# A first adaLN half in two quarters: the start of a decoder trunk layer on one Trainium2 core

## The chip, the core and the metric

The kernel runs on one core of a Trainium2 chip. A core has five engines with a queue of instructions each: TensorE (PE in the profile, its weight loads PEld), VectorE (DVE), ScalarE (ACT), GpSimd (POOL) and SyncE (SP, which here only issues DMAs). Each works through its own queue in order and waits on semaphores for the others. The metric is the device time of one execution in microseconds, the median of several runs.

## The reference

One layer of a decoder trunk, for a prompt of 512 tokens and 8 samples of one token that share the weights, all in f32:

```
sh1, sc1, g1, sh2, sc2, g2 = split(silu(c) @ ada_w + ada_b, 6)     # adaLN: 1024 -> 6 x 1024, 9 condition rows
h = rms_norm(x, norm1_g) * (1 + sc1) + sh1
xr, gr, q, k, v, fl, ga, gb = split(h @ w_in)
ya = (RG-LRU(conv(xr)) * gelu(gr)) @ w_proj_a
yb = attention_with_forget_gates(q, k, v, fl) @ w_proj_b           # samples: over a paged cache
x = x + g1 * ((sigmoid(ga) * ya + sigmoid(gb) * yb) @ w_o)
x = x + g2 * SwiGLU(rms_norm(x, norm2_g) * (1 + sc2) + sh2)
y = rms_norm(x, normf_g)
```

What matters here is the beginning: nothing of `h @ w_in` can start before the columns of sh1 and sc1 that belong to the first rows of h are known.

## The kernel before

Activations lie transposed: a tile holds 128 of the 1024 features on the partitions and all 520 tokens along the free axis, so x, xn and h are eight tiles each (f = 0 to 7). A product is made in two halves of 260 tokens (j = 0, 1). To reach f32 accuracy with the faster fp32r matmul, weights and activations are split into a high part (a cast on ACT: whi, hh) and a rest (a subtraction on DVE: wlo, hl), and three matmuls are summed for each k step: whi x hh, wlo x hh, whi x hl. A k step is one of the eight feature tiles.

The engines' queues are filled by a list scheduler that takes the program's instructions in the order of the code and moves them by its own estimate of when each is ready; `issue_after` and the tile pools' buffers set further bounds. The queues that come out are fixed; on the chip each engine works through its own in order.

The start of the kernel, in the order of the code:

1. x is loaded by SP (eight DMAs), ACT squares it, DVE adds the squares, PE sums them over the partitions (ss), ACT and DVE make 1/rms from it (r1).
2. `first_mod(0, ...)`: the first half of sh1 and sc1 (feature tiles 0 to 3 of both). For each of the eight k steps kq, SP loads 512 KB of ada_w (araw, a tile of the pool `pgp` with 7 buffers), and PE does four matmuls of 32 stationary columns (silc, the silu of the conditions) with 256 moving columns. The four write to four groups of 32 partitions of one bank, with `tile_position=(0, 32 * g)`. They are plain f32, and in the profile each shows as two instructions. From the third step on, `keep_busy` puts one full matmul with no use (idle) behind each step.
3. DVE makes xn = x * r1, eight tiles.
4. `q_weights`: SP loads a piece of q's weights (wraw), ACT and DVE split it. A piece is four k steps of two of q's output tiles.
5. `first_mod_end(0, ...)`: ACT copies the sums (adas), PE transposes them (adaft), with three idle matmuls behind it, and DVE adds the bias (mod) and makes the amplitude (n1amp).
6. `first_h(f)` for f = 0 to 3: ACT makes hh, POOL the eight sample columns, DVE the exact value (hr) and the rest hl.
7. q's first six output tiles over k steps 0 to 3, in two groups of three (`g3`), six banks each. In the first group the second adaLN half (`first_mod(1, ...)`) is put in two steps at a time behind each k step. Behind the first k step of the second group stands `first_mod_end(1, ...)` and `first_h` for f = 4 to 7.
8. Three more pieces of q's weights, then k steps 4 to 7 of the six tiles (L542 `q` in the profile, against `qp` for the steps before), and the rest of the kernel, the first parts of which load pages of the cache for the samples.

The hh and hl of tiles 4 to 7 and the last pieces of q's weights go through the same queues of ACT and DVE. The split weights (whi, wlo) have three buffers each, the pieces as loaded (wraw) two.

Of the kernel before, what the change touches and what calls it, by code (L numbers as in the profile page):

```python
# [8 lines left out]
F32 = mybir.dt.float32  # L9
# [3 lines left out]
ALU = mybir.AluOpType  # L13
# [11 lines left out]
KT = 8  # L25
# [10 lines left out]
P_N1, P_N2, P_NF, P_CW, P_CB, P_BR, P_BI, P_LAM = 0, 1, 2, 3, 7, 8, 9, 10  # L36
P_AB, P_SC, P_H0, P_C = 11, 17, 41, 49
# [28 lines left out]
def kernel(ctx, tc, xT, par, gates, b_f, cst, cse, own, cache_k, cache_v, cache_lf, pt,  # L66
# [3 lines left out]
    pe, act, dve, pool, sp = nc.tensor, nc.scalar, nc.vector, nc.gpsimd, nc.sync  # L70
# [9 lines left out]
    def slot(name, cols=NT, dt=F32, parts=128):  # L80
        return heap.tile([parts, cols], dt, name=name, tag="slot")

    def bank(name, parts=128, cols=512):
        return psp.tile([parts, cols], F32, name=name, tag="bank")
# [19 lines left out]
    ident = cs[:, C_ID:C_ID + 128]  # L104
# [371 lines left out]
    def first_mod(fh, acc, kqs):  # L476
        for kq in kqs:
            raw = pgp.tile([128, 2, 512], F32, name="araw", tag="pg")
            sp.dma_start(raw, ada_w[kq * 128:kq * 128 + 128, :2048].rearrange("p (v c) -> p v c", v=2)
                         [:, :, 512 * fh:512 * fh + 512])  # L480
            for g in range(4):
                m = pe.matmul(acc[32 * g:32 * g + 32, :256], lhsT=silc[:, kq],
                              rhs=raw[:, g // 2, 256 * (g % 2):256 * (g % 2) + 256],
                              start=kq == 0, stop=kq == KT - 1, tile_position=(0, 32 * g))
            if fh == 0:
                keep_busy(m, 1 if kq > 1 else 0)

    def keep_busy(m, n):
        for _ in range(n):
            with tc.issue_after(m.ins):  # L490
                m = pe.matmul(idle[:, :HALF], lhsT=ones, rhs=x[0][:, :HALF], start=True, stop=True)
# [53 lines left out]
    def wraw():  # L545
        return wp.tile([128, KT, 256], F32, name="wraw", tag="wraw", bufs=2)
# [3 lines left out]
    for f in range(KT):  # L550
# [6 lines left out]
        if f % 4 == 3:  # L557
            for j, (t0, t1) in enumerate(HALVES):
                pe.matmul(ssq[j][:, :HALF], lhsT=ones, rhs=sq[:, t0:t1], start=f == 3, stop=f == KT - 1)
    acc = [bank(f"adaf{fh}") for fh in range(2)]  # L560
    first_mod(0, acc[0], range(KT))
    r1 = slot("r1")
    for j, (t0, t1) in enumerate(HALVES):
        act.activation(r1[:, t0:t1], ssq[j][:, :HALF], AF.Sqrt, bias=eps, scale=1.0 / D)
        dve.reciprocal(r1[:, t0:t1], r1[:, t0:t1])
    for f in range(KT):
        t = slot("xn")
        dve.tensor_tensor(t, x[f], r1, ALU.mult)
        xn.append(t)
    raw = wraw()  # L570
    q_weights(0, raw, 0, 0)
    first_mod_end(0, acc[0])
    for f in range(4):
        first_h(f)
    q_weights(0, raw, 4, 2)
    raw = wraw()
    q_weights(0, raw, 0, 4)
    for g3 in (0, 3):
        banks = [bank(f"qp{i}_{j}") for i in range(g3, g3 + 3) for j in range(2)]
        for k in range(4):  # L580
            for n in range(6):
                q_matmuls(0, g3 + n // 2, n % 2, k, banks[n])
                if g3 == 0 and n == 5:
                    first_mod(1, acc[1], (2 * k, 2 * k + 1))
            if g3 and k == 0:
                first_mod_end(1, acc[1])
                for f in range(4, KT):
                    first_h(f)
        for n in range(6):
            t0, t1 = HALVES[n % 2]  # L590
            act.copy(qpart[g3 + n // 2][:, t0:t1], banks[n][:, :HALF])
        if g3 == 0:
            flr = slot("flr", KT * H).rearrange("p (k c) -> p k c", k=KT)
            sp.dma_start(flr, w_in[:, COL_FL:COL_FL + H].rearrange("(k p) c -> p k c", p=128))
# [1199 lines left out]
```

## Time and profile before

| | us |
|---|---|
| median of 3 runs | 1015.64 (1015.08 to 1018.36) |
| the profiled execution, its own time | 1018.03 |
| its span in the profile | 1016.4 |
| PE busy | 994.3 (98%) |
| DVE busy | 797.3 (78%) |
| ACT busy | 547.5 (54%) |
| POOL busy | 327.6 (32%) |
| first q matmul starts | 26.08 |
| first matmul of q's k steps 4 to 7 starts | 50.45 |

A row of the timeline gives start, duration, engine, line, operation, output<-inputs, shapes and a count of merged instructions; in brackets stands how long the engine had been idle and what released it. PE's ends are modelled, and its instructions overlap, so a distance between starts says more than a duration.

### The profile page before, as it was taken

The page shows a single profiled execution, that of the slowest core. Times are in us where ns is not written, and L with a number is a line of the kernel's source. Part 1 is how long each engine was busy: PE and PEld are TensorE (multiplying, and loading weights), DVE is VectorE, ACT ScalarE, POOL GpSimd, SP SyncE. Part 2 cuts the span into 40 slices and gives each one's busy share as a digit, 9 for nine tenths or more (in the row PEclk, how much of TensorE's full clock was granted, in tenths as well). Part 3 has the DMA queues.
Part 4 walks back from the last instruction along what each step waited for, and adds up shares of the span by engine and source line. Part 5 has one row for each costly group of instructions (what it writes and reads, how often), then busy time and mean ns, then how long its engine had stood idle before and what let it go on. Part 6 is the DMA issues. An engine that isn't in the chain of part 4 may idle for free.

```text
span 1016.4 us, 21281 instructions
## 1 busy us (share of the span) xinstructions
PE 994.3 (98%) x8012; PEld 921.1 (91%) x8012; DVE 797.3 (78%) x1423; ACT 547.5 (54%) x1128; POOL 327.6 (32%) x415
## 2 busy tenths in 40 slices
PE   5999999999999999999999999999999999999996
PEld 2799999999998988888888888999999999999996
DVE  5559999998999888886655544869988888888764
ACT  4534576848761576777783233554444444445553
POOL 0346111121143245653400001583442442425112
PEclk9999999999999999999999999999999999999998
DMA  9798857788879998995867995324234243233122
GB/s 325 250 324 279 242 189 202 243 261 278 281 250 345 331 312 286 321 294 190 251 216 269 319 340 186 84 74 115 81 108 125 63 125 98 70 104 105 63 64 85
DMA packets 164378, 206.97 MB, mean 204 GB/s; under 512 B 9827, under 2 KB 125043, under 8 KB 164211
## 3 DMA queue, kind: packets, MB, share of 16 engines
q1 hardware_dynamic: 147634, 152.78, 48.1%
q0 software_dynamic: 12960, 46.41, 13.8%
q10 hardware_dynamic: 3680, 6.42, 1.7%
q8 instruction: 63, 1.03, 0.4%
q14 instruction: 41, 0.33, 0.1%
HBM read 192.49 MB, written 13.09 MB: 202 GB/s over the span
## 4 chain that ended last, share of the span: by engine, by line
PE 93%; DMA 2%; DVE 2%; ACT 1%; issue 0%; SPq 0%; POOL 0%; DVEq 0%; POOLq 0%; ACTq 0%
PE fo L307 12%; PE k L307 5%; PE wo L307 5%; PE gb L307 5%; PE gr L307 5%; PE v L307 5%; PE ga L307 5%; PE xr L307 5%; PE pb L307 4%; PE pv L839 3%; PE pa L307 3%; PE po L1302 2%; PE qp L542 2%; PE q L542 2%; PE ada L374 2%; PE ptt L1268 2%
## 5 line engine op out<-in xcount | busy, mean ns | idle before, releaser
L246 ACT CAST whi<-wraw 128x1024 fp32r<-128x1024 f32 (+1 forms) x79 | 82.0, 1039 | 113.6 <-PE pb L307 34.3
L248 DVE TENSOR_TENSOR wlo<-wraw,whi 128x1024 fp32r<-128x1024 f32 (+1 forms) x79 | 99.1, 1256 | 19.0 <-ACT whi L246 16.6
L307 PE MATMUL fo<-ach,wb 128*128 128x260 f32 x512 | 93.4, 283 | 0.0
L270 ACT CAST wb<-ws 128x512 fp32r<-128x512 f32 x72 | 44.7, 621 | 86.0 <-PE fo L307 58.9
L700 POOL DMA_DIRECT2D pg<-in_cache_k_dram x74 | 39.6, 536 | 143.1 <-DVE S L751 62.6
L271 DVE TENSOR_TENSOR wb<-wraw,wb 128x512 fp32r<-128x512 f32 x86 | 76.4, 889 | 4.7 <-ACT wb L270 3.9
L307 PEld LDWEIGHTS fo<-ach,wb 128*128 128x128 f32 x512 | 78.9, 188 | 0.0
L271 DVE TENSOR_TENSOR wb<-ws,wb 128x512 fp32r<-128x512 f32 x72 | 68.7, 954 | 12.6 <-ACT wb L270 11.0
L261 POOL TENSOR_TENSOR ws<-wraw 128x512 f32<-128x512 f32 x18 | 24.4, 1353 | 153.2 <-DMA wraw<-in_w_fi_dram 104.1
L307 PE MATMUL fo<-acl,wb 128*128 128x260 f32 x256 | 72.2, 282 | 0.0
L270 ACT CAST wb<-wraw 128x512 fp32r<-128x512 f32 x86 | 53.5, 622 | 31.4 <-ACT cp L1683 6.2
L750 DVE TENSOR_TENSOR pg<-pg,qb 128x1024 f32<-128x1024 f32 x48 | 57.9, 1221 | 2.5 <-DMA pg<-in_cache_k_dram 2.5
L751 DVE TENSOR_REDUCE S<-pg 128x16 f32<-128x1024 f32 x48 | 57.4, 1209 | 0.2
L1259 POOL TENSOR_SCALAR p<-p,mu 128x128 f32<-128x128 f32 (+3 forms) x28 | 38.4, 1381 | 53.0 <-DVE mu L1255 47.1
L307 PEld LDWEIGHTS fo<-acl,wb 128*128 128x128 f32 x256 | 48.2, 188 | 0.0
L1253 ACT ACTIVATE p<-p,mu 128x128 f32<-128x128 f32 (+3 forms) x64 | 35.4, 554 | 18.2 <-DVE mu L1252 18.0
L307 PE MATMUL v<-hh,whi 128*128 128x260 f32 x128 | 38.2, 298 | 0.8 <-ACT row L819 0.5
L307 PE MATMUL k<-hh,whi 128*128 128x260 f32 x128 | 37.3, 292 | 0.0
L307 PE MATMUL pb<-oh,whi 128*128 128x260 f32 x128 | 37.1, 290 | 0.2 <-ACT oh L1360 0.2
L307 PE MATMUL gb<-hh,whi 128*128 128x260 f32 x128 | 37.0, 289 | 0.0
L307 PE MATMUL v<-hl,whi 128*128 128x260 f32 x128 | 36.9, 288 | 0.0
L307 PE MATMUL v<-hh,wlo 128*128 128x260 f32 x128 | 36.9, 288 | 0.0
(1101 smaller groups left out, 3957.3 us busy)
## 6 DMA issues: line engine op xcount, KB each, us to landing
araw<-in_ada_w_dram SPq DMA_DIRECT2D x48, 512.0 KB, 7.6
wraw<-in_w_fi_dram SPq DMA_DIRECT2D x44, 512.0 KB, 5.3
pg<-in_cache_k_dram POOLq DMA_DIRECT2D x42, 512.0 KB, 6.2
pg<-in_cache_v_dram SPq DMA_DIRECT2D x42, 512.0 KB, 5.5
wraw<-in_w_in_dram SPq DMA_DIRECT2D x34, 512.0 KB, 6.4
wraw<-in_w_in_dram SPq DMA_DIRECT2D x11, 1024.0 KB, 8.5
pg<-in_cache_v_dram POOLq DMA_DIRECT2D x22, 512.0 KB, 6.1
pg<-in_cache_k_dram POOLq DMA_DIRECT2D x32, 256.0 KB, 5.9
```

Of the source, the lines that this page charges most:

```text
L246: state["act"] = act.copy(hi[:, :k1 - k0], src)
L248: state["last"] = dve.tensor_tensor(lo[:, :k1 - k0], src, hi[:, :k1 - k0].bitcast(F32), ALU.subtract)
L270: state["act"] = act.copy(t[:, :4], src)
L271: state["last"] = dve.tensor_tensor(t[:, 4:], src, t[:, :4].bitcast(F32), ALU.subtract)
L307: state["mm"] = pe.matmul(out[:, :t1 - t0], lhsT=wt[k], rhs=at, start=k == 0 and m == 0, stop=k == nk - 1 and m == 2)
L542: state["mm"] = pe.matmul(b[:, :HALF], lhsT=wt, rhs=at[:, t0:t1], start=k == 0 and m == 0, stop=k == 3 and m == 2)
L700: done.append(eng.dma_start(pg, cache[bass.ds(r, 1), :, c0:c1].rearrange("a p c -> (a p) c")))
L750: dve.tensor_tensor(pg, pg, q, ALU.mult)
L751: last = dve.tensor_reduce(S[r // 2][:, c:c + H], pg.rearrange("p (h d) -> p h d", d=DH), AX.X, ALU.add)
L839: pe.matmul(pv[0][32 * gq:32 * gq + 32, :], lhsT=pw[r][:, c:c + 32], rhs=pgs[gq // 2][:, 512 * hf:512 * hf + 512], start=j == 0, stop=j == ...
L1253: act.activation(p[:, :n + 128], p[:, :n + 128], AF.Exp, bias=mu[:, 0:1], scale=-1.0, accum_out=mu[:, 1:2])
L1259: (pool.tensor_scalar(p, p, mu[:, 2:3], None, ALU.mult) if a and i + 1 < KT else act.activation(p, p, AF.Copy, scale=mu[:, 2:3]))
```

## The change

The first adaLN half is computed in two quarters (feature tiles 0 and 1, then 2 and 3). `quarter(fq, acc, ks)` loads, for each of four pairs of k steps, one buffer with two DMAs of 256 KB, and does two matmuls a k step instead of four, for sc1 and sh1 of 256 features; the first quarter keeps its idle matmuls. `quarter_end` does what `first_mod_end` does, for two feature tiles. Of xn only tiles 0 and 1 are made ahead of the first quarter's end, the other six behind the first two h. The first group of q (three tiles) takes k steps 0 and 1, with the second quarter in four pieces among them; then come the second quarter's end, h of tiles 2 and 3, the third piece of q's weights, and k steps 2 and 3. The second half (`first_mod(1, ...)`) is put in two steps at a time behind k steps 2 and 3 of the first group and 0 and 1 of the second, and its end stands behind k step 1 of the second group instead of 0.

```diff
--- before.py
+++ after.py
@@ -485,6 +485,37 @@
             if fh == 0:
                 keep_busy(m, 1 if kq > 1 else 0)
 
+    def quarter(fq, acc, ks):
+        for k2 in ks:
+            raw = pgp.tile([128, 2, 2, 256], F32, name="araw", tag="pg")
+            for n in range(2):
+                r0 = (2 * k2 + n) * 128
+                sp.dma_start(raw[:, n], ada_w[r0:r0 + 128, :2048].rearrange("p (v c) -> p v c", v=2)
+                             [:, :, 256 * fq:256 * fq + 256])
+            for n in range(2):
+                kq = 2 * k2 + n
+                for v in range(2):
+                    m = pe.matmul(acc[32 * v:32 * v + 32, :256], lhsT=silc[:, kq], rhs=raw[:, n, v],
+                                  start=kq == 0, stop=kq == KT - 1, tile_position=(0, 32 * v))
+                if fq == 0:
+                    keep_busy(m, 1 if kq > 1 else 0)
+
+    def quarter_end(fq, acc):
+        sb = slot("adas", 256, parts=64)
+        act.copy(sb, acc[:64, :256])
+        tp = bank(f"adaq{fq}")
+        for b in range(2):
+            m = pe.transpose(tp[:, 64 * b:64 * b + 64], sb[:, 128 * b:128 * b + 128], ident[:64, :64])
+        if fq == 0:
+            keep_busy(m, 3)
+        tv = tp[:, :128].rearrange("p (b v c) -> p b v c", b=2, v=2)
+        fs = slice(2 * fq, 2 * fq + 2)
+        for v in (1, 0):
+            dve.tensor_tensor(mod[:, v, fs], tv[:, :, v, 0:9],
+                              prm[:, fs, P_AB + v:P_AB + v + 1].to_broadcast([128, 2, 9]), ALU.add)
+        dve.scalar_tensor_tensor(amp1[:, fs], mod[:, 1, fs], 1.0, prm[:, fs, P_N1:P_N1 + 1].to_broadcast([128, 2, 9]),
+                                 ALU.add, ALU.mult)
+
     def keep_busy(m, n):
         for _ in range(n):
             with tc.issue_after(m.ins):
@@ -557,33 +588,46 @@
         if f % 4 == 3:
             for j, (t0, t1) in enumerate(HALVES):
                 pe.matmul(ssq[j][:, :HALF], lhsT=ones, rhs=sq[:, t0:t1], start=f == 3, stop=f == KT - 1)
-    acc = [bank(f"adaf{fh}") for fh in range(2)]
-    first_mod(0, acc[0], range(KT))
+    accq = [bank(f"adaf{fq}") for fq in range(2)]
+    quarter(0, accq[0], range(4))
     r1 = slot("r1")
     for j, (t0, t1) in enumerate(HALVES):
         act.activation(r1[:, t0:t1], ssq[j][:, :HALF], AF.Sqrt, bias=eps, scale=1.0 / D)
         dve.reciprocal(r1[:, t0:t1], r1[:, t0:t1])
-    for f in range(KT):
+    def scaled(f):
         t = slot("xn")
         dve.tensor_tensor(t, x[f], r1, ALU.mult)
         xn.append(t)
+
+    scaled(0)
+    scaled(1)
     raw = wraw()
     q_weights(0, raw, 0, 0)
-    first_mod_end(0, acc[0])
-    for f in range(4):
+    quarter_end(0, accq[0])
+    for f in range(2):
         first_h(f)
     q_weights(0, raw, 4, 2)
-    raw = wraw()
-    q_weights(0, raw, 0, 4)
+    for f in range(2, KT):
+        scaled(f)
     for g3 in (0, 3):
         banks = [bank(f"qp{i}_{j}") for i in range(g3, g3 + 3) for j in range(2)]
         for k in range(4):
             for n in range(6):
                 q_matmuls(0, g3 + n // 2, n % 2, k, banks[n])
-                if g3 == 0 and n == 5:
-                    first_mod(1, acc[1], (2 * k, 2 * k + 1))
-            if g3 and k == 0:
-                first_mod_end(1, acc[1])
+                if g3 == 0 and k < 2 and n % 3 == 2:
+                    quarter(1, accq[1], (2 * k + n // 3,))
+                if n == 5 and (g3 == 0) == (k > 1):
+                    c = 2 * (k - 2) if g3 == 0 else 4 + 2 * k
+                    first_mod(1, accf, (c, c + 1))
+            if g3 == 0 and k == 1:
+                quarter_end(1, accq[1])
+                for f in range(2, 4):
+                    first_h(f)
+                raw = wraw()
+                q_weights(0, raw, 0, 4)
+                accf = bank("adafh")
+            if g3 and k == 1:
+                first_mod_end(1, accf)
                 for f in range(4, KT):
                     first_h(f)
         for n in range(6):
```

Line numbers move: the matmul of `first_mod` stays L482, that of `quarter` is L498, q's is L573 instead of L542, the idle one L522 instead of L491. In the rows of the queues, names carry the number of their buffer; `128x260` is the shape of the output.

The first stage on PE. Before (adaf0 is the first half's bank; x4 are the four matmuls of a step):

```order
L482 MATMUL adaf0_143<-araw_192,silc_99 32x256 x4
L491 MATMUL idle_114<-x_79,cs_75 128x260
L498 MATMUL adaft0_230<-cs_75,adas_228 128x128 x2
L491 MATMUL idle_114<-x_79,cs_75 128x260 x3
L542 MATMUL qp0_0_286<-hh_240,whi_222 128x260
```

Now (adaf0 is the first quarter's bank):

```order
L498 MATMUL adaf0_143<-araw_170,silc_99 32x256 x2
L522 MATMUL idle_114<-x_79,cs_75 128x260
L508 MATMUL adaq0_198<-cs_75,adas_196 128x64 x2
L522 MATMUL idle_114<-x_79,cs_75 128x260 x3
L573 MATMUL qp0_0_242<-hh_208,whi_190 128x260
```

The number of steps and of idle matmuls is the same; a step has two matmuls instead of four.

PE around the second quarter's end, now (adaf1: second quarter; adaq1: its transposes; adafh: second half; qp0 to qp5: q's tiles, first three in the first group; hh_208 and hh_217 are of feature tiles 0 and 1, hh_321 of tile 2):

```order
L573 MATMUL qp2_1_247<-hl_218,whi_226 128x260
L498 MATMUL adaf1_144<-araw_305,silc_99 32x256 x4
L508 MATMUL adaq1_314<-cs_75,adas_312 128x64 x2
L482 MATMUL adafh_344<-araw_363,silc_99 32x256 x4
L482 MATMUL adafh_344<-araw_369,silc_99 32x256 x4
L573 MATMUL qp3_0_413<-hh_208,whi_226 128x260
L573 MATMUL qp3_0_413<-hh_208,wlo_227 128x260
L573 MATMUL qp3_0_413<-hl_209,whi_226 128x260
L573 MATMUL qp3_0_413<-hh_217,whi_226 128x260
L573 MATMUL qp0_0_242<-hh_321,whi_190 128x260
L573 MATMUL qp0_0_242<-hh_321,wlo_191 128x260
```

Before, a piece of the second half with four matmuls stood behind each ten or so matmuls of q, and its transposes had q matmuls ahead and behind:

```order
L482 MATMUL adaf1_144<-araw_406,silc_99 32x256 x4
L542 MATMUL qp5_0_424<-hl_241,whi_282 128x260
L542 MATMUL qp5_1_425<-hh_240,whi_282 128x260
L542 MATMUL qp5_1_425<-hh_240,wlo_283 128x260
L542 MATMUL qp5_1_425<-hl_241,whi_282 128x260
L498 MATMUL adaft1_446<-cs_75,adas_444 128x128 x2
L542 MATMUL qp3_0_420<-hh_249,whi_276 128x260
```

So the transposes now follow the quarter's last step directly, and behind them come two steps of the second half and four matmuls of the other group.

DVE at the last h tiles. Before (hr and hl of feature tiles 4 to 7, from hl of tile 4 on, with the second set of q's weight pieces, wlo, among them; the last row adds up a q tile):

```order
L519 TENSOR_TENSOR hl_454<-hr_452,hh_453 128x520
L517 TENSOR_SCALAR hr_461<-xn_214,n1amp_113,mod_102 128x512
L533 TENSOR_TENSOR wlo_551<-wraw_548,whi_550 128x1024
L519 TENSOR_TENSOR hl_463<-hr_461,hh_462 128x520
L517 TENSOR_SCALAR hr_470<-xn_216,n1amp_113,mod_102 128x512
L519 TENSOR_TENSOR hl_472<-hr_470,hh_471 128x520
L517 TENSOR_SCALAR hr_479<-xn_218,n1amp_113,mod_102 128x512
L519 TENSOR_TENSOR hl_481<-hr_479,hh_480 128x520
L533 TENSOR_TENSOR wlo_556<-wraw_548,whi_555 128x1024
L929 TENSOR_TENSOR qp_107<-q0_0_586,qp_107 128x260
```

Now:

```order
L550 TENSOR_TENSOR hl_489<-hr_487,hh_488 128x520
L548 TENSOR_SCALAR hr_496<-xn_236,n1amp_113,mod_102 128x512
L550 TENSOR_TENSOR hl_498<-hr_496,hh_497 128x520
L548 TENSOR_SCALAR hr_505<-xn_238,n1amp_113,mod_102 128x512
L564 TENSOR_TENSOR wlo_573<-wraw_565,whi_572 128x1024
L550 TENSOR_TENSOR hl_507<-hr_505,hh_506 128x520
L548 TENSOR_SCALAR hr_514<-xn_240,n1amp_113,mod_102 128x512
L564 TENSOR_TENSOR wlo_579<-wraw_576,whi_578 128x1024
L550 TENSOR_TENSOR hl_516<-hr_514,hh_515 128x520
L973 TENSOR_TENSOR qp_107<-q0_0_603,qp_107 128x260
```

The last two pieces of q's weights stood beside and behind the last hl; now the second and the third of them stand ahead of it.

## The prediction

> **What bounds the kernel now.** I read the page first, for the engine that sets the end.
>
> ```profile
> span 1016.4 us, 21281 instructions
> PE 994.3 (98%) x8012; PEld 921.1 (91%) x8012; DVE 797.3 (78%) x1423; ACT 547.5 (54%) x1128; POOL 327.6 (32%) x415
> PE 93%; DMA 2%; DVE 2%; ACT 1%; issue 0%; SPq 0%; POOL 0%; DVEq 0%; POOLq 0%; ACTq 0%
> ```
>
> TensorE (PE) is busy for 98% of the span and is 93% of the chain that ended last. So the questions are whether PE starts its useful stream earlier, and whether it gets more to do. The busy time by stretches (columns: stretch, its length, PE busy, granted clock, DMA share, GB/s), and the longest waits of PE after 100 us:
>
> ```profile
> 14.90:23.80 8.90, 8.90 (x76) 1.00 1.06 378
> 26.00:50.40 24.40, 24.21 (x211) 1.00 0.74 251
> 50.40:100.00 49.60, 49.60 (x407) 1.00 0.89 299
> PE v L307 <- ACT row L819: 0.5, 2, 0.3
> PE pv L839 <- DMA pg<-in_cache_v_dram: 0.4, 1, 0.4
> ```
>
> After 100 us the listed waits of PE are 0.5 us and below. Nothing later has the slack to take back microseconds that the start loses or to use up those it wins: what the first 60 us gain or lose is the result, within about 1 us. I therefore read the start in the timeline, PE first.
>
> ```profile
> L482 PE MATMUL adaf<-araw,silc x128: 379/403/636, 15.0 to 42.8; 128*32 128x256 f32 x128
> 21.94 0.64 PE L482 MATMUL adaf<-araw,silc 128*32 128x256 f32 x8
> 22.51 0.70 PE L491 MATMUL idle<-x,cs 128*128 128x260 f32 x2
> 23.15 0.64 PE L482 MATMUL adaf<-araw,silc 128*32 128x256 f32 x8
> 23.72 0.70 PE L491 MATMUL idle<-x,cs 128*128 128x260 f32 x2
> 24.28 0.44 PE L498 MATMUL adaft<-cs,adas 128*128 128x128 f32 x2
> 24.55 1.48 PE L491 MATMUL idle<-x,cs 128*128 128x260 f32 x6
> 26.08 0.39 PE L542 MATMUL qp<-hh,whi 128*128 128x260 f32 x1
> ```
>
> Each f32 matmul of the program is two PE instructions here. Two things are to be seen. First, the adaLN steps come every 1.21 us (21.94, 23.15) with the placeholder matmul (idle) right between them: PE itself sets this pace. The last step's weights were there earlier:
>
> ```profile
> 16.10 0.37 SPq L479 DMA_DIRECT2D araw<-in_ada_w_dram  x1
> araw<-in_ada_w_dram SPq DMA_DIRECT2D x1, 512.0 KB, 5.9
> ```
>
> Issued at 16.10, landed 5.9 us later at 22.0, used at 23.15: 1.1 us to spare. Second, one instruction lasts 0.40 us, yet eight are over in 0.64 us: four run side by side (one for each 32-column group) in a wave, and the second wave starts 0.24 us after the first. The idle matmuls, one at a time, are 0.22 us apart: (1.48 - 0.38) / 5. **A wave of four costs PE what a single instruction costs.**
>
> The link from the last step to q is on other engines:
>
> ```profile
> 23.85 0.37 ACT L495 COPY adas<-adaf 128x256 f32<-128x256 f32 x1 [8.31 <-PE adaf L482]
> 24.12 1.14 ACT L532 CAST whi<-wraw 128x512 fp32r<-128x512 f32 x2
> 24.98 0.20 DVE L508 SCALAR_TENSOR_TENSOR n1amp<-mod,prm 128x36 f32<-128x36 f32 x1
> 25.22 0.81 ACT L514 ACTIVATE hh<-xn,mod,n1amp 128x512 fp32r<-128x512 f32 x1
> 26.59 1.05 ACT L532 CAST whi<-wraw 128x1024 fp32r<-128x1024 f32 x1
> ```
>
> Copy, transposes, mod, n1amp, hh: 2.2 us from the copy to q's first matmul at 26.08.
>
> **The change part by part.**
>
> *First quarter: start of q.* It has eight steps as before, each with two matmuls instead of four, so still two waves, and the same six idle matmuls follow them. Half the bytes land sooner, but nobody waited for them. The steps keep their 1.21 us and end at 23.8. The wraw loads come earlier, and ACT does one 1024-wide cast between the copy and hh; that cast ends at about 24.12 + 1.05 = 25.17, beside mod and n1amp (done at 25.18), so it is hidden; without that cover it would cost up to 1.05. The narrower transposes and mod give perhaps 0.1. Term: -0.1 us.
>
> *More blocks inside the q stream.* What a step costs inside q is read here:
>
> ```profile
> 35.22 0.64 PE L482 MATMUL adaf<-araw,silc 128*32 128x256 f32 x8
> 35.79 0.39 PE L542 MATMUL qp<-hl,whi 128*128 128x260 f32 x1
> 37.05 0.42 PE L482 MATMUL adaf<-araw,silc 128*32 128x256 f32 x4
> 44.15 6.46 PE qp L542 x54
> ```
>
> A q matmul takes 6.46 / 54 = 0.12 us. From 35.22 to 37.05 is one step and ten q matmuls: 1.83 - 1.20 = 0.63 us for a step. Before, eight such steps stand in the stream: 5.04 us. Now there stand eight steps of the second quarter and eight of the second half. They come two by two; the second step of a pair adds two waves of 0.22, so a pair costs 0.63 + 0.44 = 1.07. Four pairs for the half: 4.28. Four for the second quarter, one of them broken by three q matmuls (another 0.63): 4.91. Together 9.19 instead of 5.04: **+4.15 us on PE**, with no wait of PE after 31 us to hide it. Per matmul nothing is added to the first half, but its array is now half empty.
>
> On exactly this point the Trainium skill, page "TensorE: Matmul & The Clock Gate", section "Measured speedup vs the span model", speaks against the change too: its model has packed tiles share one matmul's time, about 4 ns for each further tile. Its own table there gives only 3.07x for four tiles; if two shared perfectly and four did not, then 32 waves at 0.24 x 0.30 / 1.30 = 0.055 us less would be 1.8 us off, an estimate from that table, and the time 1019.5. The rows here (0.24 for four, 0.22 for one) allow 32 x 0.02 = 0.6 us, and I keep to them, inside the range.
>
> *Second end.* quarter_end(1) adds two transposes, 24.55 - 24.28 = 0.27 us. They follow directly on the quarter's last step, and nothing is put between: as at the first end of before, PE would go on 0.57 after the step's start (23.15 + 0.57 = 23.72) but the transposes start at 24.28, a wait of 0.56. Behind the transposes, two steps of the second half and four q matmuls cover mod, n1amp and hh of tile 2 (1.8 us); then hh's last columns and hl of tile 2 are some 0.4 late (hr, cast and hl as at the first tile; between 0 and 0.8).
>
> *DVE and DMA.* Six of the eight xn move behind the second h:
>
> ```profile
> 18.16 4.97 DVE L568 TENSOR_TENSOR xn<-x,r 128x520 f32<-128x520 f32 x8
> araw<-in_ada_w_dram SPq DMA_DIRECT2D x48, 512.0 KB, 7.6
> ```
>
> That is 6 x 0.62 = 3.7 us from about 28.9; with the following wlo DVE is free at about 34. The second quarter's mod is wanted at about 37, since PE needs until then for two k steps and four pairs. So it is hidden, 3 us to spare. SP issues 16 small araw loads, and the second half's loads wait for buffers that PE frees at 29 to 38; with the 7.6 us to landing of the second row they are there from 37 to 46, ahead of their pairs at about 43, 46 and 49.
>
> *Old waits at the start of q.* Before, PE from 26.08 to 50.45 takes 24.37 us for 144 x 0.12 = 17.3, the steps' 5.04 and transposes of 0.25: 1.8 us are waits, such as this (load queue of PE):
>
> ```profile
> 30.62 0.54 PEld L542 LDWEIGHTS qp<-hl,whi 128*128 128x128 f32 x4 [0.41 <-DVE hr L517]
> 50.45 0.28 PE L542 MATMUL q<-hh,whi 128*128 128x260 f32 x1
> ```
>
> The new blocks fill most of them; about 0.6 stays around the first hh. So waits go from 1.8 to 0.6 + 0.56 + 0.4 = 1.56. PE reaches q's second half at 50.45 + (4.15 + 0.27 - 0.24 - 0.1) = 54.5, 4.1 us late.
>
> *Last h tiles.* The second half's end moves two k steps back, so less of q stands behind it: 4 + 30 matmuls instead of 4 + 54.
>
> ```profile
> 42.58 0.64 PE L482 MATMUL adaf<-araw,silc 128*32 128x256 f32 x8
> 43.29 0.37 ACT L495 COPY adas<-adaf 128x256 f32<-128x256 f32 x1 [2.67 <-PE adaf L482]
> 44.65 0.55 DVE L517 TENSOR_SCALAR hr<-xn,n1amp,mod 128x512 f32<-128x512 f32 x1
> 46.66 1.23 DVE L533 TENSOR_TENSOR wlo<-wraw,whi 128x1024 fp32r<-128x1024 f32 x1
> 47.81 0.69 DVE L519 TENSOR_TENSOR hl<-hr,hh 128x520 fp32r<-128x520 f32 x1
> 50.33 0.70 DVE L519 TENSOR_TENSOR hl<-hr,hh 128x520 fp32r<-128x520 f32 x1
> ```
>
> Before, the copy starts 0.71 after the last step's start, hr of tile 4 1.36 later, and the last hl is done 6.38 after that (51.03), one wlo of 1.15 (46.66 to 47.81) among it; PE wants it at 50.45 + 11 x 0.12 = 51.8, just behind. In the new order two wlo stand ahead of the last hl. The last pair starts 1.07 + 0.27 + 34 x 0.12 = 5.4 before 54.5, at 49.1; the copy at 49.1 + 0.71 + 0.44 = 50.25, hr at 51.6, the last hl done at 51.6 + 6.38 + 1.15 = 59.1. PE has 25 matmuls to do without it, until 57.5. **A new wait of 1.6 us** (0 if the engines overlap better, 2.6 if the casts' own wait for weight buffers, which PE frees only at 54.5, stretches the line by a further cast). Later work keeps its order, so all of it moves.
>
> *Sum:* 4.1 + 1.6 = +5.7 us. The profiled execution took 1018.03 (span 1016.4), so 1023.7 of its kind; it lies 2.4 above the median of the three runs, 1015.64, for which the sum gives **1021.3 us**.
>
> **The rivals.**
> (a) *Not slower: PE is charged per matmul, not per wave.* Then a wave of two costs 0.11 instead of 0.22, and the two quarters' 32 waves are 3.5 us cheaper, half of it ahead of q: 5.7 - 3.5 = +2.2, 1017.8. It decides wherever a quarter's steps come nearer than 1.1 us in the first stage. Against it: 0.24 for four, 0.22 for one.
> (b) *Not slower: the landing sets the pace after all.* The loads of the first stage have the DMA engines to themselves from the last x on:
>
> ```profile
> PE ss L559 <- DMA x<-in_xT_dram: 10.2, 1, 10.2
> ```
>
> From 10.2 to 22.0 land 4.2 MB, at the 378 GB/s of the first stretch 11.1 us; half of that is 5.5 us sooner, and if the stage ended 1.8 us after its last landing (22.0 to 23.8) q would start so much earlier: 5.7 - 5.5 = +0.2, 1015.8. Against it: the even 1.21 us with PE busy 8.90 of 8.90.
> (c) *Slower still: waits multiply.* ACT's casts of weights stand ahead of hh of tiles 6 and 7 and wait for PE; with 2.6 for the last h and the waits of the second end doubled, +8.2, 1023.8.
> (d) *The half-empty array keeps the clock low.* The first 24 instructions of before take 2.79 us where warm ones would take half:
>
> ```profile
> 14.96 2.79 PE L482 MATMUL adaf<-araw,silc 128*32 128x256 f32 x24
> ```
>
> If the slow pace lasted through the first quarter, its 5.5 us from 18.3 on would double: 5.7 + 5.5 = +11.2, 1026.8. The idle matmuls fill the whole array, which speaks against it.
>
> **How the numbers follow.** The forecast, with its own range from 1018.7 (no wait for the last h, second end covered: 5.7 - 1.6 - 1.0 = +3.1) to 1022.3, has a chance of 0.70; (a) 0.07, (b) 0.05, (c) 0.11, (d) 0.03; 0.04 is left for a gain that I do not see. A measurement of this kernel tells about 0.3%, 3 us, from no change: the forecast and (c), (d) lie above, (a) and (b) within. Slower 0.84, same 0.12, faster 0.04. The range takes the forecast and (c), with some tenths for the spread of runs: 1018.2 to 1024.2.
>
> **What would show it.** Right: q's first matmul again near 26.0; the adaLN matmuls of a quarter in waves of two, 0.22 to 0.24 us apart; q's second half starting near 54.5; a wait of PE for hl of DVE of 1 to 2 us near 58; the same waits as before after 100 us. Wrong: q's first matmul at 22 to 24 (then b, or with shorter waves a), or no wait near 58 and the second half before 53.

## The result, and the profile after

The changed kernel takes 1024.04 us (median of 4 runs, 1023.47 to 1024.85) against 1016.09 (1015.08 to 1018.36) of the kernel before on the same chip: ratio 1.0071, 95% interval 1.0057 to 1.0086. It is slower by 7 to 8 us; the forecast was 1021.3, its range to 1024.2. The profiled execution took 1024.24. Four executions in the experiments below took 1206 to 1720 us at a mean granted clock of 0.56 to 0.75, and the ratios leave them out.

First the page of the changed kernel (span; busy time of the engines; the chain that ended last by engine):

```profile
span 1022.5 us, 21297 instructions
PE 999.2 (98%) x8014; PEld 923.7 (90%) x8014; DVE 796.0 (78%) x1426; ACT 548.6 (54%) x1129; POOL 325.5 (32%) x415
PE 92%; DMA 2%; DVE 2%; ACT 1%; issue 1%; SPq 1%; POOL 0%; DVEq 0%; POOLq 0%; ACTq 0%
```

PE is busy 4.9 us longer (999.2 against 994.3), of a span that is 6.1 us longer: most of the loss is work, the rest waiting. The timeline of PE shows where. First the end of the first stage, then the second quarter's end, then the last h:

```profile
21.57 0.62 PE L498 MATMUL adaf<-araw,silc 128*32 128x256 f32 x4
22.76 0.63 PE L498 MATMUL adaf<-araw,silc 128*32 128x256 f32 x4
25.61 0.39 PE L573 MATMUL qp<-hh,whi 128*128 128x260 f32 x1
25.84 0.28 PE L573 MATMUL qp<-hh,wlo 128*128 128x260 f32 x1
26.80 0.39 PE L573 MATMUL qp<-hh,whi 128*128 128x260 f32 x1 [0.68 <-ACT hh L549]
...
35.37 1.06 PE L498 MATMUL adaf<-araw,silc 128*32 128x256 f32 x8
36.89 0.33 PE L508 MATMUL adaq<-cs,adas 64*128 64x64 f32 x2 [0.47 <-ACT adas L505]
37.16 1.07 PE L482 MATMUL adafh<-araw,silc 128*32 128x256 f32 x16
...
55.16 0.28 PE L573 MATMUL q<-hh,whi 128*128 128x260 f32 x1
58.33 0.28 PE L573 MATMUL q<-hl,whi 128*128 128x260 f32 x1
59.30 0.51 PE L573 MATMUL q<-hl,whi 128*128 128x260 f32 x2 [0.69 <-DVE hl L550]
```

A step of the first quarter (4 instructions where 8 were) still lasts 0.62 us, and the steps come every 1.19 us (21.57, 22.76). A pair of the second quarter (8 instructions, 35.37) lasts 1.06 us, one of the second half (16 instructions, 37.16) 1.07: half the matmuls, the same time. q starts at 25.61 (26.08 before), and q's k steps 4 to 7 at 55.16, where it was 50.45. At 58.33 PE runs out of work that needs no late hl, and at 59.30 it goes on.

The waits of PE from 20 to 115 us (total, times, longest) are these three; the rows of VectorE at the last h follow:

```profile
PE q L573 <- DVE hl L550: 0.7, 1, 0.7
PE qp L573 <- ACT hh L549: 0.7, 1, 0.7
PE adaq L508 <- ACT adas L505: 0.5, 1, 0.5
```

```profile
55.21 1.22 DVE L564 TENSOR_TENSOR wlo<-wraw,whi 128x1024 fp32r<-128x1024 f32 x1
56.35 0.69 DVE L550 TENSOR_TENSOR hl<-hr,hh 128x520 fp32r<-128x520 f32 x1
56.96 0.54 DVE L548 TENSOR_SCALAR hr<-xn,n1amp,mod 128x512 f32<-128x512 f32 x1
57.41 1.22 DVE L564 TENSOR_TENSOR wlo<-wraw,whi 128x1024 fp32r<-128x1024 f32 x1
58.55 0.69 DVE L550 TENSOR_TENSOR hl<-hr,hh 128x520 fp32r<-128x520 f32 x1
```

The two wlo stand ahead of the last two hl, and the last hl ends at 59.24 (51.03 before).

### The profile page after: what moved, and what is told of

It is laid out like the page before. It is cut to its first block, busy times and chain, and to the rows that moved or that the text cites. A ratio compares the mean times of both kernels' runs of the same rounds, so it can differ in the third digit from the quotient of the medians.

```text
span 1022.5 us, 21297 instructions
## 1 busy us (share of the span) xinstructions
PE 999.2 (98%) x8014; PEld 923.7 (90%) x8014; DVE 796.0 (78%) x1426; ACT 548.6 (54%) x1129; POOL 325.5 (32%) x415
## 4 chain that ended last, share of the span: by engine, by line
PE 92%; DMA 2%; DVE 2%; ACT 1%; issue 1%; SPq 1%; POOL 0%; DVEq 0%; POOLq 0%; ACTq 0%
PE fo L307 12%; PE k L307 5%; PE wo L307 5%; PE gb L307 5%; PE gr L307 5%; PE ga L307 5%; PE xr L307 5%; PE pb L307 4%; PE v L307 4%; PE pv L883 3%; PE pa L307 3%; PE po L1346 2%; PE ada L374 2%; PE ptt L1312 2%; PE qp L573 1%; PE q L573 1%
## 5 line engine op out<-in xcount | busy, mean ns | idle before, releaser
L271 DVE TENSOR_TENSOR wb<-ws,wb 128x512 fp32r<-128x512 f32 x72 | 63.2, 877 | 12.7 <-ACT wb L270 11.1
L1297 ACT ACTIVATE p<-p,mu 128x128 f32<-128x128 f32 (+3 forms) x64 | 35.3, 553 | 18.0 <-DVE mu L1296 17.7
```

Source lines behind the costliest of these rows:

```text
L271: state["last"] = dve.tensor_tensor(t[:, 4:], src, t[:, :4].bitcast(F32), ALU.subtract)
L1297: act.activation(p[:, :n + 128], p[:, :n + 128], AF.Exp, bias=mu[:, 0:1], scale=-1.0, accum_out=mu[:, 1:2])
```

## The experiments

Unless said otherwise a median is of 6 to 12 runs, and each ratio is to the kernel before on the same chip (medians 1016.47, 1017.45, 1016.88 and 1016.95 in the four groups below). "First product" is the first matmul behind q (xr): 87.09 us before, 93.04 after. "pa" is a later product: 296.93 and 302.93.

**Group 1: what a half-empty wave costs, the last h, and a packed form.**

*e0_after*, the changed kernel again.

> The changed kernel itself, unchanged, beside the kernel before on this chip, for the others of this call to be read against. Its profile had a span 6.1 us longer than that of before, its median was 7.95 us longer (four runs each, those of before spread over 3.3 us). Theory: the true difference is what the spans show, 6.1 us (5.5 to 7). Rival: something outside the first 60 us adds another 2 us, and the median difference stays at 8.

1023.59 us, ratio 1.0072 (1.0057 to 1.0087): 7.1 us above the median of before, between the 6.1 of the theory and the 8 of the rival. q started at 24.86, q's k steps 4 to 7 at 54.42: from q's start to there 29.56 us, where the first run took 29.55 (25.61 to 55.16). The start moves with the moment at which the granted clock becomes full (15.8 us here, 17.0 in the first run, 17.7 in the run of before); distances from q's start do not. I use those from here on.

*e1_fill*: the unused column groups get two more matmuls a step.

```diff
+                for v in range(2):
+                    m = pe.matmul(acc[64 + 32 * v:96 + 32 * v, :256], lhsT=silc[:, kq], rhs=raw[:, n, v],
+                                  start=kq == 0, stop=kq == KT - 1, tile_position=(0, 64 + 32 * v))
```

> The changed kernel with the two unused column groups of every step of both quarters filled: two more matmuls a step, with the same operands, into the unused partitions 64 to 127 of the same bank (their sums are not read). So 32 more matmuls of the program, 64 on PE. Theory (a wave costs what one instruction costs, however many groups it fills): no change against the changed kernel, within 0.5 us; q's first matmul again near 25.8, q's k steps 4 to 7 again at 55.2. Rival (PE is charged per matmul): 16 steps x 2 waves x 0.11 us = 3.5 us slower.

1022.58 us, ratio 1.0061 (1.0039 to 1.0082), and 29.04 us from q's start to its k steps 4 to 7: not longer. That it is 0.5 us shorter does not come from the waves: in this kernel's queue the wlo that stood ahead of the first h is done earlier (it starts at 20.79 instead of 24.78), and the wait of 0.68 us for the first hh is absent (group 4 says why). The second quarter's blocks, with the wait ahead of their transposes, take 5.11 us instead of 5.03. In its timeline L498 is the old pair of groups, L501 the added one:

```profile
34.81 0.39 PE L498 MATMUL adaf<-araw,silc 128*32 128x256 f32 x2
34.83 0.39 PE L501 MATMUL adaf<-araw,silc 128*32 128x256 f32 x2
35.03 0.39 PE L498 MATMUL adaf<-araw,silc 128*32 128x256 f32 x2
35.24 0.39 PE L498 MATMUL adaf<-araw,silc 128*32 128x256 f32 x2
```

Waves follow each other by 0.21 to 0.22 us with four groups filled, as with two. **Rival (a) falls: a wave has one price, however many of its groups work.** The quarters therefore pay for twice the array that they use. The profiled execution of this kernel still took 1025.39 us: its first product came 0.5 us sooner behind q's start (66.92 us against 67.43), but at 106 us PE waited 1.6 us for a wlo of VectorE.

*e2_late*: the second and third piece of q's weights for k steps 4 to 7 behind the last hh and hl.

```diff
...
-            state["act"] = act.copy(hi[:, ks], src[:, ks])
-            state["last"] = dve.tensor_tensor(lo[:, ks], src[:, ks], hi[:, ks].bitcast(F32), ALU.subtract)
+            with tc.issue_after(state["hc"].ins) if fh and i else nullcontext():
+                state["act"] = act.copy(hi[:, ks], src[:, ks])
+            with tc.issue_after(state["hl"].ins) if fh and i else nullcontext():
+                state["last"] = dve.tensor_tensor(lo[:, ks], src[:, ks], hi[:, ks].bitcast(F32), ALU.subtract)
...
```

(The lines not shown keep the last hh's cast and the last hl in `state["hc"]` and `state["hl"]`.)

> The changed kernel with the second and third piece of q's weights for k steps 4 to 7 cast and subtracted behind the last hh and the last hl instead of ahead of them; nothing else moves. Theory (PE waits at 58 to 59 for the last hl because two wlo and a cast stand ahead of it): hl of tile 7 is done 2.2 us sooner, PE's wait there of 1.4 us goes, about 1.4 us faster than the changed kernel. Rival (the wait is set by the second half's end, not by the pieces, or turns into one for the delayed pieces): 0.3 us or less.

1023.9 us, ratio 1.0075 (1.0059 to 1.0091): nothing gained. The wait for hl went as expected, and the first product came 36.65 us behind the start of q's k steps 4 to 7 (87.09 - 50.45 = 36.64 before, 37.87 to 37.88 in the changed kernel). The two longest waits of this kernel, and its VectorE just ahead of the new one:

```profile
PE xr L307 <- DVE wlo L248: 1.1, 1, 1.1
PE qp L575 <- ACT hh L549: 0.7, 1, 0.7
```

```profile
82.15 2.48 DVE L792 TENSOR_TENSOR pg<-pg,qb 128x1024 f32<-128x1024 f32 x2 [3.92 <-DMA qb<-qtd]
84.56 2.33 DVE L793 TENSOR_REDUCE S<-pg 128x16 f32<-128x1024 f32 x2
86.81 2.79 DVE L792 TENSOR_TENSOR pg<-pg,qb 128x1024 f32<-128x1024 f32 x2
89.52 2.33 DVE L793 TENSOR_REDUCE S<-pg 128x16 f32<-128x1024 f32 x2
91.78 1.21 DVE L248 TENSOR_TENSOR wlo<-wraw,whi 128x1024 fp32r<-128x1024 f32 x1
```

VectorE waits 3.92 us for a small load (qb, the samples' q read back from memory), works 9.6 us on key products, and only then makes the wlo that PE wants. That wait takes back in this run what the first gave.

*e3_pack*: a quarter computes two k steps side by side in the four groups; the second matmul operand of the end (fold) adds the two while it transposes. One idle matmul is left behind each of two pairs.

```diff
...
-                    m = pe.matmul(acc[32 * v:32 * v + 32, :256], lhsT=silc[:, kq], rhs=raw[:, n, v],
+                    g = 2 * n + v
+                    m = pe.matmul(acc[32 * g:32 * g + 32, :256], lhsT=silc[:, 2 * k2 + n], rhs=raw[:, n, v],
...
-            m = pe.transpose(tp[:, 64 * b:64 * b + 64], sb[:, 128 * b:128 * b + 128], ident[:64, :64])
+            m = pe.matmul(tp[:, 64 * b:64 * b + 64], lhsT=sb[:, 128 * b:128 * b + 128], rhs=fold, start=True, stop=True)
...
```

> The changed kernel with both k steps of a pair side by side in the four column groups: even k steps in groups 0 and 1, odd ones in 2 and 3; a quarter is then four steps of four matmuls instead of eight of two. The two partial sums are added by PE in the step that transposes, with a matrix of two stacked identities instead of the identity. Idle matmuls only behind the second and third step of the first quarter. Theory (the changed kernel's loss is its half-filled waves): the first stage loses four of its eight steps and q starts near 21.5 instead of 25.8; in the q stream a quarter costs 4 x 0.63 = 2.5 us instead of 4.9; together 5 to 7 us faster than the changed kernel, 1016 to 1018, about the time before. Rival (the stage is bound by DMA landing, or by DVE's reciprocal, xn and the xn moved behind): under 3 us.

1020.6 us, ratio 1.004 (1.0026 to 1.0055): 3 us better than the changed kernel, where 5 to 7 were expected, and still 4 worse than before. q starts at 21.76, 4.3 us earlier than before, yet its k steps 4 to 7 start at 50.15, only 0.3 earlier. Against the changed kernel the second quarter's blocks, with the wait ahead of their transposes, fall from 5.03 to 2.84 us, as forecast. But the second half's rise from 4.00 to 4.68, the second quarter's transposes from 0.27 to 0.59, and the first product comes 38.91 us behind the start of q's k steps 4 to 7 instead of 37.87. From q's start to the first product it is 67.30 us against 67.43, so the 3 us are the earlier start (21.76 against 24.86 in e0_after) and nothing else. The waits (PE, from 20 to 115 us):

```profile
PE adaq L510 <- ACT adas L507: 1.5, 2, 1.0
PE q L575 <- DVE hl L552: 1.2, 2, 0.9
PE qp L575 <- ACT hh L551: 0.6, 1, 0.6
```

**Group 2: parts of the change taken out.**

*e4_skip*: three pairs of the second quarter without matmuls.

```diff
+            if fq and k2 in (1, 2, 3):
+                continue
...
```

> The changed kernel with the matmuls of three of the second quarter's four pairs of k steps left out (their loads stay, so the sums of that quarter are incomplete). If the blocks inside the stream of q cost PE what the forecast says (0.63 + 0.44 = 1.07 us a pair), q's k steps 4 to 7 start 3.2 us sooner than in the changed kernel (about 51.5) and the median falls by about as much, to about 1020.5. If the blocks fill waits that are there anyway, q's second half moves by less than 1.6 us. If only the last h sets the time, the wait there grows by what the blocks give and the median stays at 1023.6.

1022.7 us, ratio 1.0055 (1.004 to 1.007). From q's start to its k steps 4 to 7 it took 27.83 us instead of 29.55: 1.7 gained, where 3.2 or less than 1.6 was expected. Summed over the distances between PE's starts, the quarter's matmuls fell from 4.50 to 1.53 us, near the 3.2 forecast, and the wait of 0.53 ahead of the transposes went as well, but the matmuls of the second half rose from 4.00 to 5.94. Without the cover, PE waits for the first hh of tile 2, which was hidden before (0.8 us), and the pairs of the half are broken up into more pieces:

```profile
PE q L575 <- DVE hl L552: 1.3, 2, 0.9
PE qp L575 <- ACT hh L547: 0.8, 1, 0.8
PE qp L575 <- ACT hh L551: 0.7, 1, 0.7
```

So the blocks cost their full length on PE (2.97 us for three pairs), and of the 3.5 us that their absence and that of the wait gave, 1.9 came back at the next places.

*e5_early*: the second half is not moved back.

```diff
-                if n == 5 and (g3 == 0) == (k > 1):
-                    c = 2 * (k - 2) if g3 == 0 else 4 + 2 * k
+                if g3 == 0 and k > 1 and n % 3 == 2:
+                    c = 4 * (k - 2) + 2 * (n // 3)
                     first_mod(1, accf, (c, c + 1))
...
-            if g3 and k == 1:
+            if g3 and k == 0:
                 first_mod_end(1, accf)
```

> The changed kernel with one part undone: the second half is not moved back. Its four pairs stand behind n = 2 and n = 5 of k steps 2 and 3 of the first group, and its end and the last four h behind k step 0 of the second group, as before. The forecast's fifth step: the wait of PE for the last hl (57.7 to 59.3) goes, since 18 more q matmuls (2.2 us) and two pairs stand behind the end; q's k steps 4 to 7 start at 54.5 as in the changed kernel, the first product behind q comes at 91.6 instead of 93.0, and the median is 1.4 us lower, about 1022.2. Rival, as seen when the weight pieces were put behind the last hl: VectorE is full from 80 to 105 us, PE waits there for wlo, 1 us or more, and the median stays at 1023.6.

1022.16 us, ratio 1.0048 (1.0033 to 1.0063). The wait for hl is gone from the list, and the first product comes 36.56 us behind the start of q's k steps 4 to 7 (37.87 after). That start is 0.6 us later from q's own start (30.15 us): the half's blocks stand in more pieces (4.28 us in place of 4.00), and q's matmuls with their waits take 20.40 in place of 20.08. The waits:

```profile
PE qp L573 <- ACT hh L549: 0.7, 1, 0.7
PE adaq L508 <- ACT adas L505: 0.5, 1, 0.5
PE ga L307 <- DVE wlo L248: 0.3, 1, 0.3
```

**The late end of the second half, with two wlo ahead of the last hl, made the wait at 58 us**: without the one (here) or the other (e2_late) it is gone. By the ratios this is worth 2.4 us, by the trace 0.7 (q's start to the first product, 66.71 against 67.43). The spans of the two profiled runs differ by 2.1 us (1021.9 and 1019.8): 0.5 is there at pa (302.33 and 301.85), and most of the rest is a stretch at half clock near 465 us, worth 1.7 us, which e0_after's profiled run has and this one has not (last section). The intervals of the two ratios overlap, so the size of the step stays between 0.7 and 2.4 us.

*e6_packearly*: e3_pack with the same edit.

> The packed quarters (two k steps side by side) together with the second half not moved back. If the 2.3 us that the packed kernel lost between q's second half and the first product behind it were the wait for the last h alone, the median falls from 1020.6 to 1018.3, still 2 us above the kernel before: the second end, the four pairs of the second quarter in the stream (4 x 0.63 = 2.5 us that nothing covers) and the waits around the first h use up the earlier start of q. If the start of q at 21.8 were worth its full 4.3 us, it would be 1013 or less. If VectorE's stretch from 80 us on takes the gain back, 1020.6.

1019.21 us, ratio 1.0016 (1.0004 to 1.0028): the best form with quarters, between the 1018.3 and the 1020.6 of the forecast, and still slightly slower than before. Its first product came at 87.65, 1.4 earlier than in e3_pack, but then PE waited:

```profile
PE adaq L510 <- ACT adas L507: 1.9, 2, 1.5
PE xr L309 <- DVE wlo L250: 1.2, 1, 1.2
```

and pa came at 299.36, 211.71 us behind the first product, where before takes 209.84 and the changed kernel 209.89.

*e7_fewer*: the kernel before without two idle matmuls.

```diff
-                keep_busy(m, 1 if kq > 1 else 0)
+                keep_busy(m, 1 if kq in (2, 3, 4, 7) else 0)
```

> The kernel before, with the idle matmul behind two of its adaLN steps (kq 5 and 6) left out. If PE sets the pace of the first stage by its own length (1.21 us a step, 0.64 of it the idle matmul) down to the landing of the last step's weights at 22.0 us, q starts about 1.1 us sooner (25.0 instead of 26.08), q's second half at about 49.4, and the median is 1.1 lower, about 1015.4. If the landing sets the pace, q starts where it did, and the time is that of before. If the idle matmuls are what keeps the clock up there, the granted clock falls below 1 between 20 and 26 us and the time is 1 us or more longer.

1016.62 us, ratio 0.9991 (0.9979 to 1.0003): not to be told from before; 1.1 us less was one of the forecasts. The granted clock stayed at 1.00 from 20 to 26 us. Its first stage:

```profile
20.37 1.14 PE L482 MATMUL adaf<-araw,silc 128*32 128x256 f32 x16
22.26 0.64 PE L482 MATMUL adaf<-araw,silc 128*32 128x256 f32 x8 [0.74 <-DMA araw<-in_ada_w_dram]
25.64 0.39 PE L542 MATMUL qp<-hh,whi 128*128 128x260 f32 x1 [0.49 <-ACT hh L514]
```

The last step starts at 22.26 instead of 23.15, now held by its load, and q at 25.64. Of the 0.9 us at the last step q got 0.4, and a wait for wlo at 87 us (0.7) took more than that back before pa (297.81, where before has 296.93).

**Group 3: is VectorE's order what takes gains back?** One edit, on e7_fewer (*e8_fewer_keys*), on e6_packearly (*e9_packearly_keys*) and on the kernel before (*e10_before_keys*):

```diff
-        state["age"] = 1 if state["n"] < 5 else 2
+        state["age"] = 2
```

> The kernel before with two idle matmuls left out, and the first key products one product later on VectorE, so that the two wlo of the first product behind q stand ahead of the four key instructions that wait for a small load (qb). If VectorE's order there is what took back the earlier start, the wait of PE for wlo at 87 us goes, the first product behind q starts at 86.9, pa at about 296.7 instead of 297.8, and the median falls from 1016.6 to about 1015.5, 1 to 2 us below the kernel before. If VectorE's total work from 80 to 110 us is the bound, not its order, the wait comes back at a later wlo and the time stays at 1016.6.

> The packed quarters with the second half not moved back, and the first key products one product later on VectorE. If VectorE's order took back the gain there (PE waited 1.2 us for wlo at 88 us, and 1.9 us more than the kernel before between the first product behind q and pa), the median falls from 1019.2 to 1017.3, about the kernel before; what is left is the second end and the broken pairs. If its total work is the bound, 1019.2.

> The kernel before with only the first key products one product later on VectorE: what that edit does by itself. In the profiled run of before PE had no wait for wlo near 87 us, so by the order theory nothing is there to win in such a run, at most some tenths in runs where the small load comes late: 1016.5 to 1017.4. If the pages' buffers, held longer by the later key products, delay the loads of weights, the time is 1 us or more longer.

In none of the three traces does PE wait at the first product (in the profiled run of before it did not either), and pa follows it by 210.00 us (e8; 210.95 without the edit), 210.19 (e9; 211.71) and 210.36 (e10; 209.84). But the medians did not fall: 1017.65 (ratio 1.0009, 0.9999 to 1.002), 1019.38 (1.003, 1.0018 to 1.0042) and 1017.82 (1.0008, 0.9997 to 1.0018). In e8_fewer_keys, whose start is that of e7_fewer, q started at 26.62, since the last load came a microsecond later:

```profile
21.86 0.64 PE L482 MATMUL adaf<-araw,silc 128*32 128x256 f32 x8 [0.66 <-DMA araw<-in_ada_w_dram]
23.23 0.64 PE L482 MATMUL adaf<-araw,silc 128*32 128x256 f32 x8 [0.73 <-DMA araw<-in_ada_w_dram]
```

So VectorE's order explains the wait, but not that it costs a median anything. What the edit loses elsewhere stays open, and no version tried here is faster than the kernel before by more than the noise.

**Group 4: the wait around the first hh.** *e11_port*: in the changed kernel the second wlo behind the first two hl.

```diff
...
-            state["last"] = dve.tensor_tensor(lo[:, ks], src[:, ks], hi[:, ks].bitcast(F32), ALU.subtract)
+            with tc.issue_after(state["hl"].ins) if (fh, i) == (0, 2) else nullcontext():
+                state["last"] = dve.tensor_tensor(lo[:, ks], src[:, ks], hi[:, ks].bitcast(F32), ALU.subtract)
```

> The changed kernel with the wlo of the second piece of q's weights put behind the first two hl on VectorE instead of ahead of them. In the changed kernel GpSimd's first hr, which takes 0.20 us elsewhere, took 1.27 us beside that wlo (1.22 us, started 0.01 us earlier), and PE waited 0.68 us for hh's last columns. If VectorE's long two-input operation holds GpSimd up, the first hr takes 0.2 to 0.6 us, the wait goes, the first matmul of q's k steps 4 to 7 starts 28.9 to 29.1 us behind q's first instead of 29.55, and the median falls by 0.5, to about 1023. If the first instruction on GpSimd is slow by itself, hr takes 1.2 us again and the distance stays at 29.55.

GpSimd's first hr, first in the changed kernel (with VectorE's row beside it), then here:

```profile
24.78 1.22 DVE L564 TENSOR_TENSOR wlo<-wraw,whi 128x1024 fp32r<-128x1024 f32 x1
24.79 1.27 POOL L546 TENSOR_TENSOR hr<-xn,n1amp 128x8 f32<-128x8 f32 x1 [23.55 <-DVE n1amp L516]
```

```profile
25.46 0.20 POOL L546 TENSOR_TENSOR hr<-xn,n1amp 128x8 f32<-128x8 f32 x1 [24.23 <-DVE n1amp L516]
```

1.27 us beside the wlo, 0.20 without it, and the 0.68 us wait of PE is gone. e1_fill, whose wlo is done before, also has 0.20 and no such wait. q's start to its k steps 4 to 7 fell only from 29.55 to 29.35, since a pair of the quarter was broken once more (its matmuls, with the wait ahead of the transposes, 5.57 instead of 5.03 us). Median 1022.89, ratio 1.006 (1.0047 to 1.0074), which overlaps the changed kernel's.

## Why the prediction was right, and where its sizes were off

The direction, the mechanism and the place held. Step by step, from the traces of before and after (sums are over the distances between PE's starts from q's first matmul to its k steps 4 to 7):

| step | forecast | measured |
|---|---|---|
| q starts | -0.1 | -0.47 (26.08 to 25.61) |
| more blocks in the stream | +4.15 | +3.95 (4.55 to 8.50) |
| second transposes | +0.27 | +0.27 (0.17 to 0.44) |
| waits in the stream | -0.24 | +0.96 |
| q's k steps 4 to 7 start | +4.1 | +4.7 (50.45 to 55.16) |
| from there to the first product | +1.6 | +1.24 (36.64 to 37.88) |
| sum at the first product | +5.7 | +5.95 (87.09 to 93.04) |
| span | +5.7 | +6.1 |

- *First quarter.* It kept its pace. That q starts 0.47 earlier is mostly the clock, full 0.7 us earlier in that run, which is worth half of that; the kernel of e10_before_keys, with the start of before, has 25.64. Rivals (a) and (b) fall: (a) by e1_fill, (b) because q started 0.5 us earlier and not 5.5. But (b) was nearer than I allowed. I put 1.1 us to spare at the last load; with the idle matmuls thinned, the load held the last step at 22.26 in one run and 23.23 in another, against 23.15 before.
- *Blocks.* A pair costs 1.00 (second half, 4.00 for four) to 1.13 us (second quarter, 4.50 for four), forecast 1.07 and 1.23. The wave as the unit of price was right. Of the 1.8 us that the prediction's estimate takes off for half-filled waves next to nothing is there: with the empty groups filled (e1_fill) the second quarter's blocks are 0.08 us longer, and the steps of the first stage come every 1.21 us instead of 1.19.
- *Waits in the stream.* This step failed. I let the new blocks fill most old waits. The 0.53 ahead of the transposes came as forecast, and of the 0.4 for hh and hl of tile 2 no wait shows. But q's own matmuls with their waits grew from 19.65 to 20.08 us, because the weight split that moved ahead of the first h blocks GpSimd: without it (e11_port) they take 19.36. I had found its cast hidden on ACT and had not looked at its wlo on VectorE and at who runs beside it.
- *Last h.* The wait came at 58 us, in two pieces on PE, 1.24 in place of 1.6, and e5_early and e2_late tie it to the late end of the second half and the two wlo. Part of the difference is a miscount: I put 34 q matmuls between the last pair and q's k steps 4 to 7, and the trace has 36. Two more at 0.12 bring the forecast wait to 1.36.
- *Rivals (c) and (d).* (c) named 1023.8, close to the median, but by a mechanism that is not there: the waits of the second end did not double (0.5 us), and the last h cost less than forecast, not more. The median lies only 0.16 us inside the upper end of the range, and that end was drawn to take in (c): that 1024.04 still falls within it is luck. (d) falls: the quarter's steps come every 1.19 us at full clock.
- *After 60 us.* For this change it held that nothing adds or takes back: the first product to pa is 209.84 us before and 209.89 after. As a general statement it was wrong. In e2_late, e6_packearly and e7_fewer, which won time ahead of 80 us, VectorE held PE for 0.7 to 1.2 us near the first product, and in e1_fill for 1.6 us at 106 us. It is no rule either: e4_skip won 1.1 us up to the first product and kept it (209.42 from there to pa).
- *From the profile to the median.* Here most of the miss lies. The profiled execution of before stood 2.4 us above the median that I saw, and I let the changed kernel's stand as much above its own. It does not: 1024.24 profiled, 1024.04 median, and in e0_after 1023.51 and 1023.59. 1018.03 + 6.1 = 1024.1 is what came; my subtraction of 2.4 made 1021.3 of 1023.7. The granted clocks on record give part of the reason. The profiled run of before has the stretch at half clock near 465 us, worth 1.7 us (last section). In all fourteen profiled executions the mean clock is 0.996 or less with that stretch and 0.997 or more without it. By this mark 20 of the 68 counted runs of before in the four groups have it, with a median of 1018.25 us, and the other 48 have a median of 1016.47. Of the ten runs of the changed kernel five are on each side, with medians of 1023.84 and 1023.47. So before's profiled run was of the slower kind, and 1015.64 lies near the median of the other. Why the changed kernel's runs without the stretch are hardly faster stays open.

## What to carry to other kernels

Count packed small matmuls in waves, not in matmuls: splitting a stage in two halves its array use, not its time, unless two of its steps are packed into the wave that is left half empty. When an end moves later in an engine's stream, count the work that remains behind it and compare it with the whole chain on the other engines (here the last hl is done 9.8 us behind the start of the last pair, 49.44 to 59.24, while PE comes to its last matmul without it 8.9 us behind, at 58.33). And treat the excess of one profiled execution over the median as a property of that execution, not as an offset that the changed kernel shares; its mean clock beside those of the other runs can tell part of it.

## What the runs showed of the hardware

**A half-clock window in dense work.** Seven of the fourteen profiled executions (before, after, e0 to e3 and e8) show the granted clock at half for one stretch of 3.4 us near 465 us, where attention's small matmuls leave PE short gaps. The stretches of 3.4 us before and in it (stretch, length, PE, PEld, DVE, ACT, POOL busy, clock, DMA share, GB/s), in the changed kernel, then two stretches at about the same place of e9_packearly_keys, where it stayed away:

```profile
464.20:467.60 3.40, 2.79 (x14) 1.76 (x14) 3.33 (x8) 0.72 (x2) 0.00 (x0) 1.00 1.07 307
467.60:471.00 3.40, 3.40 (x18) 3.40 (x17) 2.60 (x13) 2.58 (x11) 0.31 (x1) 0.50 1.04 317
```

```profile
459.20:462.60 3.40, 2.89 (x17) 2.00 (x16) 3.33 (x8) 0.32 (x1) 0.00 (x0) 1.00 1.05 330
462.60:466.00 3.40, 3.40 (x27) 3.29 (x26) 2.43 (x13) 3.09 (x13) 0.81 (x2) 1.00 1.06 333
```

No single gap of PE in the stretch before is longer than 0.27 us, and the gaps together are 0.4 to 0.6 us. It costs about 1.7 us (half of 3.4). What brings it on stays open: the share of time that PE is busy does not decide. In the seven runs PE is busy for 2.79 to 2.96 us of the 3.40 before (2.96 in e0_after). In e10_before_keys it is busy for 2.90 from 460.57 to 463.97 us, in the changed kernel itself for 2.71 from 58.00 to 61.40, in e1_fill for 1.76 from 103.13 to 106.53, and behind each of these the clock stays at 1.00. The half clock began 443.73, 447.15 or 450.56 us behind the moment at which the clock became full, which itself varied from 15.5 to 18.5 us; these distances are 130, 131 and 132 times 3.413 us. The Trainium skill, page "TensorE: Matmul & The Clock Gate", section "What's actually happening", has a window of 3413 ns that runs freely; the traces agree. Its section "Why this matters for your kernels" asks for no idle gap above about 3 us; here the half clock came with no gap above 0.27 us.

**GpSimd blocked by VectorE for a whole instruction**: hr 1.27 us beside a wlo that started 0.01 us earlier, 0.20 without it (e11_port, e1_fill). In e4_skip another hr took 1.18 us beside a wlo that had started 0.11 us earlier. The Trainium skill, page "SBUF — State Buffer", section "SBUF: two separate sides", says that the two share a port pair under a lock held for the whole instruction; the rows agree.
